# Interleaved column walks in ten of the sixteen gate projections of a hybrid encoder layer

## The chip, the cores and the metric

The kernel runs on one core of one Trainium2 chip. The metric is the device time of one execution in microseconds (us), the median over several runs. Engines are named as in the profile: PE is TensorE's matmul, PEld its weight load, DVE is VectorE, ACT is ScalarE, POOL is GpSimd, SP is SyncE.

## The reference, cut to what matters

One layer over 512 tokens of width 1024: a SwiGLU half step, a mixer with two attention branches, and a second SwiGLU half step. The change touches one part of the mixer, the gates:

```
proj = h @ w_in
pa, pq, pk, pv, pg = proj[..., :o1], proj[..., o1:o2], proj[..., o2:o3], proj[..., o3:o4], proj[..., o4:]
...
gates = jax.nn.sigmoid((pg + b_gate).reshape(B, S, N_BRANCHES, D))
merged = gates[:, :, 0] * (o_a @ w_branch_a) + gates[:, :, 1] * (o_b @ w_branch_b)
return merged @ w_out
```

`pg` has 2048 features for each of the 512 tokens. The kernel makes them as sixteen tiles of 128 features by 512 tokens.

## The kernel before, in words

**Layout.** Activations lie transposed, with features on the 128 partitions and the 512 tokens along the row. The normed input `h` stands in SBUF as eight pairs of tiles `hH[k]`, `hL[k]` (128x512 each): a value rounded to fp32r and the rest, so that a product of near fp32 accuracy is made of three fp32r matmuls. `mm3` (L248 to L252) issues these three: high weights by `hH` (L250), high weights by `hL` (L251), low weights by `hH` (L252). Weights pass through `prep`, which makes a high part `wh` on ACT (L235) and a low part `wl` on DVE (L236).

**A gate projection.** `feat` (L260 to L268) takes one PSUM bank `mm` (128x512 fp32) and one chunk of weights (128x1024, eight slices of 128 columns). For each of the eight `k` it calls `mm3`, so that 24 matmuls accumulate in the bank. In each the weights' slice is the stationary operand, `hH[k]` or `hL[k]` with its 512 columns is the moving one, and the output is the whole bank. At the end `done` (L686 to L689) multiplies the bank by the token scale `R` on DVE (L688, result `z`) and stores `z` to DRAM (`gate_d`), from where it is read back much later, after the attention (L1140). `feat` also serves the first projections of the FFNs and four query/key projections; these calls pass no walk.

**Where the gates stand.** The PE's instruction order is written out by hand (a manual schedule for PE). `self.items` lists the mixer's projections: the value projection `("v", 1)`, gates 0 to 3, the query/key block, `("v", 2)`, gates 4 and 5, two query/key pairs, gates 6 to 12, the inputs of the second attention in three groups, gates 13 to 15, and the projection of the first attention's output. The items after the query/key block are a filler stream: `weave` lets the attention issue a step and then takes a number of steps from that stream, one `mm3` each. So gates 0 to 3 stand in one piece, and gates 4 to 15 are mostly cut into pieces between attention matmuls.

**Operands that are read or written with a step.** Three places of the kernel before do not walk a row from left to right without gaps. The value projections 1 and 2 use as stationary operand every fourth column of `hH` and `hL`, `t[:, r:T:4]` (128 columns, 16 bytes from one to the next). In `values_a`, stages 2 and 3, the matmuls of L912 write every fourth column of the bank, `out[:, r0 + u // 2:T:4]`, where stages 0 and 1 write 64 or 128 columns side by side. The broadcast of one column in `stat_R` (L423) has step zero. No moving operand has a step other than one.

**Alignment.** Weight tiles are placed at a chosen offset in bytes modulo 256 (`offset`, used in `ring`). For gates the weights then start at the same place modulo 256 as `hH` and `hL` do.

Of the kernel before, what the change touches and what calls it, by code (L numbers as in the profile page):

```python
# [32 lines left out]
LAG = 1  # L33
LAST = 2
WARM = 4
T = 512
D = 1024
NK = 8
# [32 lines left out]
class Layer:  # L71
    def __init__(self, ctx, tc, a):
# [10 lines left out]
        c = self.cst  # L83
        self.x = [c.tile([128, T], F32, name=f"x{d}") for d in range(NK)]
        self.par = c.tile([128, 48], F32, name="par")
# [7 lines left out]
        self.r = c.tile([128, 8], F32, name="r")  # L93
        self.R = c.tile([128, T], F32, name="R")
        nc.gpsimd.memset(self.R, 0.0)
        self.acc = c.tile([128, T], F32, name="acc")
        self.open_h()
        self.gate_d = self.dram.tile([16, 128, T], F32, name="gate_d")
        self.qk_d = self.dram.tile([2 * NSQ, 128, T], F32, name="qk_d")
        gates = lambda lo, hi: [("g", j) for j in range(lo, hi)]  # L100
# [41 lines left out]
    def open_h(self):  # L142
        self.hctx = ExitStack()
        hp = self.hctx.enter_context(self.tc.tile_pool(name="hp", bufs=1, side="right", reuse_waits="tile"))
        self.hH = [hp.tile([128, T], F32R, name=f"hH{d}") for d in range(NK)]
        self.hL = [hp.tile([128, T], F32R, name=f"hL{d}") for d in range(NK)]
# [110 lines left out]
    def aux(self, name):  # L257
        return self.psa.tile([128, T], F32, tag="aux", name=name)

    def feat(self, name, n, done):  # L260
        ps = self.bank()
        H, L = self.weights(name, n)
        for k in range(NK):
            s = slice(128 * k, 128 * k + 128)
            self.mm3(ps, H[:, s], L[:, s], self.hH[k], self.hL[k], k == 0, k == NK - 1)
            if k == NK - 1:
                done(ps)
            yield  # L268
# [390 lines left out]
    def stream(self, items):  # L659
        nc = self.nc  # L660
        for kind, n in items:
            if kind == "v":
                toks = [(lambda t, r=r: t[:, r:T:4]) if n else (lambda t, r=r: t[:, 128 * r:128 * r + 128]) for r in range(4)]

                def done(j, b, g=n):
                    rc = self.r[:, j + (4 if g else 0):j + (5 if g else 1)]
                    if j % 2:
                        nc.vector.tensor_scalar(self.V[g][:, j, :], b, rc, None, op0=ALU.mult)
                    else:
                        nc.scalar.activation(self.V[g][:, j, :], b, AF.Copy, scale=rc)  # L670

                yield from self.token("wav", 4 * n, toks, done)
            elif kind == "qk":
                hp, g = PAIRS[n]
                for part in range(2):

                    def done(ps, hp=hp, part=part, g=g):
                        t = self.qk[hp][part, g] = self.ap.tile([128, T], F32, tag="qk", name="qk", bufs=9)
                        nc.vector.tensor_mul(t.rearrange("p (r m) -> p r m", r=4),
                                             ps.rearrange("p (m r) -> p r m", r=4),  # L680
                                             self.acc.rearrange("p (r m) -> p r m", r=4))

                    yield from self.feat("waq", 2 * n + part, done)
            elif kind == "g":

                def done(ps, j=n):  # L686
                    z = self.tmp.tile([128, T], F32, tag="t", name="z")
                    nc.vector.tensor_mul(z, ps, self.R)  # L688
                    nc.sync.dma_start(self.gate_d[j], z)  # L689

                yield from self.feat("wg", n, done)
            elif kind == "pa":
                self.ma = [self.mp.tile([128, T], F32, name=f"ma{d}") for d in range(NK)]
                for d in range(NK):
                    ps = self.bank()
                    for k in range(4):
                        self.mm3(ps, *self.block("wpa", 4 * d + k), self.oH[k], self.oL[k], k == 0, k == 3)
                        if k == 3:
                            nc.scalar.copy(self.ma[d], ps)
                        yield  # L700
            else:
                toks = [(lambda t, i=i: t[:, 128 * i:128 * i + 128]) for i in range(4)]
                yield from self.token("wb", 4 * n, toks, lambda i, b, grp=n: self.rope(grp, i, b))
                self.turn()
            self.past.add((kind, n))
# [457 lines left out]
    def layer(self, out):  # L1163
# [4 lines left out]
        warm = self.aux("warm")  # L1168
        for _ in range(WARM):
            nc.tensor.matmul(warm[:, :256], self.R[:, :128], self.R[:, :256], start=True, stop=True)  # L1170
# [125 lines left out]
```

## Time and profile before

| what | value |
|---|---|
| median of 3 runs | 1258.35 us |
| lowest and highest run | 1258.33, 1259.05 us |
| span of the profiled execution | 1257.3 us |
| its time outside the span, against the median | 1258.35 - 1257.3 = 1.05 us |
| PE matmul busy | 1244.8 us, 99% of the span, 8076 rows |
| PE weight load busy | 1112.6 us, 88% |
| DVE, ACT, POOL busy | 893.0, 595.9, 122.5 us |
| mean granted TensorE clock | 0.998 |
| HBM traffic | 170.55 MB read, 15.29 MB written |

The page gives the profiled execution its span and no other time, so the median stands in for it. The duration of a matmul row reaches from its start to its modelled end and overlaps the next row; what a matmul costs a full PE is the distance from one start to the next. An fp32 matmul that is no transpose has two rows in the trace, an fp32r matmul one.

### The profile page before, as it was taken

How to read it: one execution, taken by the hardware profiler on the slowest of the kernel's cores; microseconds unless marked ns; L12 is line 12 of the kernel's file. 1: busy time of each engine (PE TensorE's matmuls, PEld its weight loads, DVE VectorE, ACT ScalarE, POOL GpSimd, SP SyncE). 2: the span in 40 equal slices, each digit the busy share in tenths (PEclk: the TensorE clock that was granted, in tenths of full speed). 3: DMA queues.
4: the chain of work that ended last, by engine and by line, in shares of the span. 5: the costliest groups of instructions: out<-in, count | busy, mean ns of one | idle time of the engine just before them, and what ended most of it. 6: DMA issues, size and time to landing. Idle time of an engine off the chain costs nothing.

```text
span 1257.3 us, 20126 instructions
## 1 busy us (share of the span) xinstructions
PE 1244.8 (99%) x8076; PEld 1112.6 (88%) x8076; DVE 893.0 (71%) x1344; ACT 595.9 (47%) x886; POOL 122.5 (10%) x128
## 2 busy tenths in 40 slices
PE   9999999999999999999999999999999999999997
PEld 7897999899899999977788878888889989988997
DVE  7784688478784887466746798866678747874874
ACT  8551355145453444444423446654475415532553
POOL 1111101000210110200000110000301000100001
PEclk9999999999999999999999999999999999999999
DMA  9875777342385973653223220147737536743222
GB/s 296 230 192 166 193 197 192 99 103 68 135 226 180 231 222 110 218 158 101 79 97 116 85 93 17 34 150 219 225 102 187 174 100 177 193 151 102 67 84 67
DMA packets 85981, 183.49 MB, mean 146 GB/s; under 512 B 12528, under 2 KB 19072, under 8 KB 85888
## 3 DMA queue, kind: packets, MB, share of 16 engines
q1 hardware_dynamic: 68048, 141.27, 33.6%
q0 software_dynamic: 17120, 40.39, 16.1%
q8 instruction: 63, 1.03, 0.4%
q10 hardware_dynamic: 720, 0.55, 0.1%
q14 instruction: 30, 0.25, 0.1%
HBM read 170.55 MB, written 15.29 MB: 148 GB/s over the span
## 4 chain that ended last, share of the span: by engine, by line
PE 96%; DVE 1%; DMA 1%; ACT 1%; SPq 0%; issue 0%; POOL 0%; DVEq 0%
PE mm L250 25%; PE mm L252 24%; PE mm L251 24%; PE Y L251 4%; PE Y L250 4%; PE Y L252 4%; PE X L251 2%; PE X L252 2%; PE X L250 2%; PE S L861 1%; PE mm L912 1%; PE Tb L1051 1%; PE T L930 1%; PE Sb L252 1%; PE Sb L251 1%; PE Sb L250 1%
## 5 line engine op out<-in xcount | busy, mean ns | idle before, releaser
L235 ACT CAST wh<-wr 128x1024 fp32r<-128x1024 f32 x139 | 145.7, 1049 | 189.5 <-PE mm L251 125.3
L236 DVE TENSOR_TENSOR wl<-wr,wh 128x1024 fp32r<-128x1024 f32 x139 | 170.7, 1229 | 43.2 <-ACT wh L235 43.0
L250 PE MATMUL mm<-hH,wh 128*128 128x256 f32 (+1 forms) x600 | 199.6, 333 | 0.2 <-ACT hH L389 0.2
L252 PE MATMUL mm<-hH,wl 128*128 128x256 f32 (+1 forms) x600 | 195.6, 326 | 1.0 <-DVE wl L236 1.0
L251 PE MATMUL mm<-hL,wh 128*128 128x256 f32 (+1 forms) x600 | 195.5, 326 | 0.3 <-DVE hL L390 0.3
L250 PE MATMUL mm<-gg,wh 128*128 128x512 f32 (+1 forms) x376 | 141.5, 376 | 0.0
L251 PE MATMUL mm<-gg,wh 128*128 128x512 f32 (+1 forms) x376 | 141.0, 375 | 0.0
L252 PE MATMUL mm<-gg,wl 128*128 128x512 f32 (+1 forms) x376 | 141.0, 375 | 0.0
L250 PEld LDWEIGHTS mm<-hH,wh 128*128 128x128 f32 x600 | 112.8, 188 | 14.6 <-issue 3.2
L252 PEld LDWEIGHTS mm<-hH,wl 128*128 128x128 f32 x600 | 112.7, 188 | 12.0 <-DVE wl L236 1.5
L251 PEld LDWEIGHTS mm<-hL,wh 128*128 128x128 f32 x600 | 112.9, 188 | 9.8 <-DVE hL L390 0.8
L235 ACT CAST wh<-wa 128x1024 fp32r<-128x1024 f32 x50 | 52.6, 1052 | 102.8 <-PE mm L251 55.4
L235 ACT CAST wh<-wt 128x1024 fp32r<-128x1024 f32 x50 | 52.6, 1052 | 71.1 <-PE mm L251 46.4
L236 DVE TENSOR_TENSOR wl<-wt,wh 128x1024 fp32r<-128x1024 f32 x50 | 61.2, 1224 | 33.2 <-ACT wh L235 32.4
L235 ACT CAST wh<-ws 128x1024 fp32r<-128x1024 f32 x50 | 52.6, 1052 | 66.6 <-PE mm L251 47.5
L250 PE MATMUL mm<-TH,wh 128*128 128x256 f32 x304 | 83.9, 276 | 0.0
L251 PE MATMUL mm<-TL,wh 128*128 128x256 f32 x304 | 83.9, 276 | 0.0
L252 PE MATMUL mm<-TH,wl 128*128 128x256 f32 x304 | 83.9, 276 | 0.0
L250 PEld LDWEIGHTS mm<-gg,wh 128*128 128x128 f32 x376 | 70.6, 188 | 14.2 <-PE mm L252 0.9
L252 PEld LDWEIGHTS mm<-gg,wl 128*128 128x128 f32 x376 | 70.6, 188 | 12.8
L251 PEld LDWEIGHTS mm<-gg,wh 128*128 128x128 f32 x376 | 70.6, 188 | 12.5
L546 DVE TENSOR_TENSOR u<-mm,R 128x512 f32<-128x512 f32 x40 | 27.6, 691 | 75.6 <-PE mm L252 75.5
(270 smaller groups left out, 3215.7 us busy)
## 6 DMA issues: line engine op xcount, KB each, us to landing
wr<-in_w2a SPq DMA_DIRECT2D x22, 512.0 KB, 3.4
wr<-in_w2b SPq DMA_DIRECT2D x22, 512.0 KB, 3.4
wt<-in_w13b SPq DMA_DIRECT2D x20, 512.0 KB, 3.4
wa<-in_w13b SPq DMA_DIRECT2D x20, 512.0 KB, 3.3
wt<-in_w13b POOLq DMA_DIRECT2D x20, 512.0 KB, 5.8
wt<-in_w13a SPq DMA_DIRECT2D x18, 512.0 KB, 3.5
wt<-in_w13a POOLq DMA_DIRECT2D x18, 512.0 KB, 6.1
wa<-in_w13a SPq DMA_DIRECT2D x18, 512.0 KB, 3.3
```

What stands on the lines that cost most here:

```text
L235: self.nc.scalar.copy(H, raw)
L236: self.nc.vector.tensor_sub(L, raw, f32(H))
L250: mm(out, lH, rH, start=start, stop=False, skip_group_check=more)
L251: mm(out, lH, rL, start=False, stop=False, skip_group_check=more)
L252: mm(out, lL, rH, start=False, stop=stop, skip_group_check=more)
L546: nc.vector.tensor_mul(u, ps, R)
L861: nc.tensor.matmul(*args, start=True, stop=True)
L912: nc.tensor.matmul(oc, v, p, start=st, stop=sp)
L930: nc.tensor.transpose(ps[:, 128 * b:128 * b + 128], P[h][:, c0 + 128 * b:c0 + 128 * b + 128], self.ident)
L1051: nc.tensor.transpose(pt[:, 128 * j:128 * j + 128], P[h, j][:, 128 * k:128 * k + 128], self.ident)
```

## The change

A table gives ten of the gates a pair (parts, run); gates 0, 5, 10, 11, 12 and 15 have none. (The title that came with the change speaks of eleven gates; the table holds ten.) For a gate with a pair, moving operand and output are handed to the matmul as the same 512 columns in another order: the row is cut into `parts` equal parts, and the walk takes `run` neighbouring columns from the first part, `run` from the second, and so on, and then the next runs. With (2, 2) the columns come in the order 0, 1, 256, 257, 2, 3, 258, 259 and so on. Both sides use one order, so that each column of the output still gets its own sum. Number and order of the instructions, weights, tiles and waits stay as they were.

```
WALK = {1: (2, 2), 2: (2, 4), 3: (2, 8), 4: (2, 16), 6: (2, 32), 7: (2, 64), 8: (4, 16), 9: (4, 4), 13: (8, 8), 14: (2, 128)}
...
+    @staticmethod
+    def walk(t, how):
+        if how is None:
+            return t
+        parts, run = how
+        return t.rearrange("p (a m c) -> p m a c", a=parts, c=run)
+
-    def feat(self, name, n, done):
+    def feat(self, name, n, done, how=None):
...
-            self.mm3(ps, H[:, s], L[:, s], self.hH[k], self.hL[k], k == 0, k == NK - 1)
+            self.mm3(self.walk(ps, how), H[:, s], L[:, s], self.walk(self.hH[k], how), self.walk(self.hL[k], how), k == 0, k == NK - 1)
...
-                yield from self.feat("wg", n, done)
+                yield from self.feat("wg", n, done, WALK.get(n))
```

On PE, at the seam between gate 1 and gate 2 (both in the first piece, before the query/key block), there stands before, output on the left of the arrow, then moving and stationary operand, then the moving operand's shape:

```order
L250 MATMUL mm<-hH_104,wh 128x512
L251 MATMUL mm<-hL_112,wh 128x512
L252 MATMUL mm<-hH_104,wl 128x512
L250 MATMUL mm<-hH_97,wh 128x512
L251 MATMUL mm<-hL_105,wh 128x512
```

and now:

```order
L251 MATMUL mm<-hH_104,wh 128x128x2x2
L252 MATMUL mm<-hL_112,wh 128x128x2x2
L253 MATMUL mm<-hH_104,wl 128x128x2x2
L251 MATMUL mm<-hH_97,wh 128x64x2x4
L252 MATMUL mm<-hL_105,wh 128x64x2x4
```

No row has moved; the 512 columns are now read as 128 times 2 parts times runs of 2 in gate 1, and as 64 times 2 times 4 in gate 2. (The line numbers inside `mm3` are one higher because the table stands above it.)

Further on, on PE in the woven part, where gate 8 ends and gate 9 begins between two steps of the first attention (L912 before, L920 now, are the products of probabilities and values), there stands before:

```order
L912 MATMUL mm<-PT,V_3443 64x128 x8
L250 MATMUL mm<-hH_104,wh 128x512
L251 MATMUL mm<-hL_112,wh 128x512
L252 MATMUL mm<-hH_104,wl 128x512
L250 MATMUL mm<-hH_97,wh 128x512
```

and now:

```order
L920 MATMUL mm<-PT,V_3443 64x128 x8
L251 MATMUL mm<-hH_104,wh 128x8x4x16
L252 MATMUL mm<-hL_112,wh 128x8x4x16
L253 MATMUL mm<-hH_104,wl 128x8x4x16
L251 MATMUL mm<-hH_97,wh 128x32x4x4
```

Here too the neighbours are the same, and only the shapes of the gate's matmuls differ. On PE 240 rows differ in this way, 24 for each of ten gates; on DVE, ACT, POOL and SP none differs.

More of the change, by code (lines that the diff above doesn't have):

```diff
@@ L35 @@
 WARM = 4
+WALK = {1: (2, 2), 2: (2, 4), 3: (2, 8), 4: (2, 16), 6: (2, 32), 7: (2, 64), 8: (4, 16), 9: (4, 4), 13: (8, 8), 14: (2, 128)}
 T = 512
```

## The prediction

> **What bounds the kernel now.** I read the page first, then PE's waits, then the places at which gates stand, and last the rows that show a step in an operand. The page says that PE is the bound:
>
> ```profile
> span 1257.3 us, 20126 instructions
> PE 1244.8 (99%) x8076; PEld 1112.6 (88%) x8076; DVE 893.0 (71%) x1344; ACT 595.9 (47%) x886; POOL 122.5 (10%) x128
> PE 96%; DVE 1%; DMA 1%; ACT 1%; SPq 0%; issue 0%; POOL 0%; DVEq 0%
> ```
>
> PE is busy for 99% of the span, and 96% of the chain that ended last is PE. PE's waits leave nothing to be won or to hide in:
>
> ```profile
> PE mm L912 <- DVE PT L932: 1.5, 1, 1.5
> PE warm L1170 <- POOL R L95: 1.3, 1, 1.3
> PE mm L252 <- DVE wl L236: 1.0, 1, 1.0
> PE rb L423 <- POOL r L407: 1.0, 1, 1.0
> PE stat L414 <- ACT sqh L624: 0.5, 1, 0.5
> PE mm L251 <- DVE PTL L158: 0.4, 1, 0.4
> PE mm L251 <- DVE hL L390: 0.3, 1, 0.3
> PE mm L250 <- ACT hH L389: 0.2, 1, 0.2
> PE Tb L1051 <- DVE Pb L1045: 0.2, 1, 0.2
> ```
>
> Together they are 6.4 us, nine waits in the whole span. So what a gate's matmul costs PE is added to the end in full, and what it saves is taken off in full.
>
> What a gate costs is read where gates 0 to 3 stand in one piece. These are DVE's rows there; each `z` starts when its gate's last matmul is done:
>
> ```profile
> 377.53 0.69 DVE L688 TENSOR_TENSOR z<-mm,R 128x512 f32<-128x512 f32 x1 [2.77 <-PE mm L252]
> 382.97 0.69 DVE L688 TENSOR_TENSOR z<-mm,R 128x512 f32<-128x512 f32 x1 [3.31 <-PE mm L252]
> 388.41 0.69 DVE L688 TENSOR_TENSOR z<-mm,R 128x512 f32<-128x512 f32 x1 [3.36 <-PE mm L252]
> 393.85 0.69 DVE L688 TENSOR_TENSOR z<-mm,R 128x512 f32<-128x512 f32 x1 [3.36 <-PE mm L252]
> ```
>
> A gate takes 5.44 us from `z` to `z`, and has 24 matmuls, so a matmul costs 5440/24 = 226.7 ns, whatever its row's duration is. That is 0.443 ns for one column of 4 bytes, and 226.7/128 = 1.77 ns for four neighbouring columns, 16 bytes of a partition. DVE waits about 3.3 us in front of each `z`, so it is no bound there.
>
> **The change part by part.** Nothing is removed or added; 240 matmuls (ten gates by 24) read and write the same columns in another order. DMAs, weights, DVE and ACT work and all waits are the same. So the sum has one price in it, the distance between such matmuls, times 240, and nothing hides it. It has three parts: the moving operand's reads, the output's writes, and how the reads stand against the next weights' load.
>
> *The reads.* The trace before has no moving operand with a step, so I take the nearest row, a stationary operand with one. In this window the weight loads of the value projection take one column out of four (16 bytes from one to the next), and beside them are weight loads without a step:
>
> ```profile
> L251 PEld LDWEIGHTS mm<-wl,hH 128*128 128x128 f32 x13 | 4.0, 311 | 0.0
> L250 PEld LDWEIGHTS mm<-wh,hH 128*128 128x128 f32 x13 | 4.0, 310 | 0.0
> L252 PEld LDWEIGHTS mm<-wh,hL 128*128 128x128 f32 x13 | 4.0, 309 | 0.0
> L251 PEld LDWEIGHTS mm<-gg,wh 128*128 128x128 f32 x10 | 1.9, 188 | 0.4
> ```
>
> The step costs 310 - 188 = 122 ns for 128 columns, 0.95 ns a column. What a column costs without a step comes from loads of fewer columns, here 8 columns and 64:
>
> ```profile
> L650 PEld LDWEIGHTS bps<-bias,rel_bias x6: 80/82/84, 101.0 to 109.5; 32*8 32x8 f32 x6
> ```
>
> ```profile
> L912 PEld LDWEIGHTS mm<-PT,V x256: 132/137/138, 558.2 to 655.9; 128*64 128x64 f32 x128
> ```
>
> From 64 to 128 columns it is (188 - 137)/64 = 0.80 ns a column, from 8 to 128 (188 - 82)/120 = 0.88 ns. With the step a column costs 0.80 + 0.95 = 1.75 to 0.88 + 0.95 = 1.83 ns. So one column out of 16 bytes takes as long as the moving operand needs for 16 whole bytes, 1.77 ns. I read this as a port that takes 16 bytes at a time, about 1.77 ns each, and a plain moving operand that is already at that limit.
>
> By this a walk pays for each visit to a new group of 16 bytes. Runs of 4 and more start at multiples of 16 bytes (`hH` and `hL` start at a multiple of 32 bytes, and the parts are 256, 512 or 1024 bytes long): such a walk visits 128 groups a matmul, as the plain one does, and costs nothing. Gate 1 alone, with runs of 2, uses half of each group and comes back later for the rest: 512/2 = 256 visits by 1.77 ns = 453 ns in place of 226.7. For its 24 matmuls that is 24 x 226.7 ns = **5.44 us** more; with 1.75 to 1.83 ns a visit, 5.3 to 5.8 us. The lower bound for gate 1 is zero, if two columns are enough to hide the next visit; a gain I exclude, since the plain order already has the fewest visits. For the other nine gates the lower bound is zero too. Their upper bound is one lost visit at every jump: their runs are 128 + 128 + 64 + 64 + 32 + 32 + 16 + 8 + 4 = 476 a matmul, times 24 times 1.77 ns = 20.2 us. I take zero, by the loads with the step, which jump at every column and still pay no more than a visit.
>
> [...]
>
> *The writes.* The nearest rows are the products of L912 in `values_a`. The first of these two is stage 0, with columns side by side, the second stage 2, with every fourth column of the bank, both accumulating:
>
> ```profile
> 558.19 1.09 PE L912 MATMUL mm<-PT,V 128*64 128x128 f32 x16
> ```
>
> ```profile
> 569.26 1.09 PE L912 MATMUL mm<-PT,V 128*64 128x128 f32 x16 [1.51 <-DVE PT L932]
> ```
>
> The same 16 rows take 1.09 us either way, so a step of 16 bytes in the output costs nothing here. These are fp32 matmuls of 128 columns, slower for each column than a gate's, so it is no proof for 0.443 ns a column. I take zero; the upper bound is a matmul of double length, as a rival below.
>
> [...]
>
> *Against the weights' load.* In the value projection the weights are read with a step while the moving operand runs plainly, and the matmuls stand a little wider:
>
> ```profile
> 354.19 0.40 PE L252 MATMUL mm<-wh,hL 128*128 128x512 f32 x1
> ...
> 357.01 0.40 PE L252 MATMUL mm<-wh,hL 128*128 128x512 f32 x1
> ```
>
> There are twelve steps between the two (the rows run L250, L251, L252 four times): 2.82/12 = 235 ns, 8 ns over a gate's 226.7. A walk changes how the moving reads stand against the next weights' reads, so it can lose as much: 0 to 240 x 8 ns = 1.9 us. I take the 72 matmuls of gates 1 to 3, which are at 226.7 ns now: 72 x 8 ns = **0.6 us**. The other seven stand among attention steps, where the distance varies already.
>
> The sum against the profiled execution is 1257.3 + 5.44 + 0.6 = 1263.3 us of span; with the 1.05 us that lie outside it, 1258.35 + 6.0 = **1264.4 us**. The later parts have no cover to lose: gate 1's DVE row and its store come 5 us later, and the next items have their weights ready, as PE's waits show none there.
>
> **The rivals.** *Two columns are enough.* Not slower than before: the port fetches the next 16 bytes while two columns are used, so that 1.77 ns a visit is a latency and not a rate. It decides in gate 1, and wins if a matmul there stays under 240 ns. For it: the stepped loads show one column a visit only, never two. Against it: plain moving columns already go at 1.77 ns for four. Time: 1258.35 + 0 to 1.9, say 1258.9 us. Chance 0.30.
>
> *Every jump costs.* The port takes more than 16 bytes ahead when a row is read in order, and a jump throws that away. Half a visit a jump, 0.89 ns x 476 x 24 = 10.1 us, beside gate 1's 5.44: 1273.9 us. For it: moving reads run in order everywhere before, so no row excludes it. Against it: the stepped loads, whose columns are at least in ascending order, show no more than a visit. Chance 0.16.
>
> *The output pays.* All ten gates write jumping at full rate, and their matmuls double: 240 x 226.7 ns = 54.4 us, 1312.8 us. For it: L912 writes fewer columns in a given time. Against it: its equal 1.09 us. Gate 14, with only four runs a matmul, would show it by itself. Chance 0.08.
>
> *The walks part the two reads better.* If the walks took away the 8 ns in the seven woven gates and cost nothing else, 168 x 8 ns = 1.3 us would go: 1257.0 us. Chance 0.04. That the walk is lost on its way to the engine can be left out, since the shapes of 240 PE rows carry it.
>
> **How the numbers follow.** My forecast has 0.42, with a range of its own from 1261 us (half of gate 1's price) to 1266.2 (5.8 and 1.9 us more). The range for 8 in 10 goes from the last rival's 1257.0 to the 1273.9 of the jumps: it holds the forecast, the first rival, the last one, and half of the jumps, 0.42 + 0.30 + 0.04 + 0.08 = 0.84, less a little at the edges. A measurement of this kernel can tell about 0.2%, 2.5 us, from no change. Faster than that would take twice the last rival's price; I give it half of that rival's chance, 0.02. Within it lie the first rival and the other half, 0.32; slower are 0.42 + 0.16 + 0.08 = 0.66.
>
> **What would show it.** Right: gate 1 takes about 10.9 us from the `z` of gate 0 to its own, gates 2 and 3 about 5.4 to 5.6 us each, and gates 4 to 15 as long as before. Wrong: gate 1 at 5.4 us means the first rival; gates 2 and 3 at rising prices for shorter runs (gate 2 at twice gate 3's surplus) mean the jumps; gate 14 longer by over 1 us means the output. PE's waits should stay where they are.

## The result, and the profile after

| | before | after |
|---|---|---|
| median of 3 runs | 1258.35 us | 1263.79 us |
| lowest and highest run | 1258.33, 1259.05 | 1263.76, 1264.39 |
| ratio, 95% interval | | 1.0042, 1.0027 to 1.0057 |
| span of the profiled execution | 1257.3 us | 1262.0 us |

The kernel is 5.44 us slower, where 6.0 was forecast. That is more than 0.2%, and the forecast lies inside the interval. The total hides two errors, though: gate 1 costs 2.7 us where 5.44 were forecast, and the other nine gates cost 2.8 us where almost nothing was. These are the lines of the page after that answer to those of before:

```profile
span 1262.0 us, 20126 instructions
PE 1249.9 (99%) x8076; PEld 1112.5 (88%) x8076; DVE 893.0 (71%) x1344; ACT 596.5 (47%) x886; POOL 122.7 (10%) x128
PE 96%; DMA 1%; ACT 1%; DVE 1%; SPq 0%; issue 0%; POOL 0%; POOLq 0%; DVEq 0%
```

The span grew by 4.7 us and PE's busy time by 5.1; the other engines' busy times moved by 0.6 us at most, and the mean granted clock is 0.998 in both. The spans differ by less than the medians do. In the profiled execution after, 1263.79 - 1262.0 = 1.8 us lie outside the span, and in the runs below it is about as much; so the 1.05 us that the median gave for before set its span against the wrong time, and the profiled execution of before was probably the 1259.05 us one. PE's longest waits after, with total, count and longest in us:

```profile
PE warm L1178 <- POOL R L96: 1.3, 1, 1.3
PE mm L920 <- DVE PT L940: 1.1, 1, 1.1
PE rb L431 <- POOL r L415: 1.0, 1, 1.0
PE mm L253 <- DVE wl L237: 1.0, 1, 1.0
```

They are the first four of nine. All nine are the same as before, 6.0 us together in place of 6.4. So no new wait came in, and the loss is in the distance between matmuls. DVE's rows for gates 0 to 3, each `z` after its gate's last matmul:

```profile
377.35 0.69 DVE L696 TENSOR_TENSOR z<-mm,R 128x512 f32<-128x512 f32 x1 [2.77 <-PE mm L253]
385.50 0.69 DVE L696 TENSOR_TENSOR z<-mm,R 128x512 f32<-128x512 f32 x1 [6.02 <-PE mm L253]
391.51 0.69 DVE L696 TENSOR_TENSOR z<-mm,R 128x512 f32<-128x512 f32 x1 [4.00 <-PE mm L253]
397.34 0.69 DVE L696 TENSOR_TENSOR z<-mm,R 128x512 f32<-128x512 f32 x1 [3.77 <-PE mm L253]
```

From `z` to `z` gate 1 takes 8.15 us, gate 2 6.01, gate 3 5.83. By 24 matmuls that is 340, 250 and 243 ns each, all from 226.7. The woven gates are read between two rows with nothing but matmuls of one gate between them. PE's rows in gate 9, walk (4, 4), before:

```profile
626.47 0.40 PE L250 MATMUL mm<-hH,wh 128*128 128x512 f32 x1
...
627.84 0.39 PE L250 MATMUL mm<-hH,wh 128*128 128x512 f32 x1
```

and after:

```profile
630.17 0.43 PE L251 MATMUL mm<-hH,wh 128*128 128x512 f32 x1
...
630.98 0.44 PE L251 MATMUL mm<-hH,wh 128*128 128x512 f32 x1
```

Before, six steps take 1.37 us, 228 ns each; after, three take 0.81 us, 270 ns each. The table gives the mean over all rows of a gate that are followed by another fp32r matmul; the last column is 24 times the difference.

| gate | walk (parts, run) | ns before | ns after | us in all |
|---|---|---|---|---|
| 1 | (2, 2) | 226.7 | 339.2 | 2.70 |
| 2 | (2, 4) | 226.7 | 250.5 | 0.57 |
| 3 | (2, 8) | 226.7 | 243.3 | 0.40 |
| 4 | (2, 16) | 252.8 | 260.5 | 0.18 |
| 6 | (2, 32) | 238.8 | 246.4 | 0.18 |
| 7 | (2, 64) | 246.5 | 246.2 | -0.01 |
| 8 | (4, 16) | 243.8 | 245.5 | 0.04 |
| 9 | (4, 4) | 238.5 | 275.6 | 0.89 |
| 13 | (8, 8) | 231.2 | 253.1 | 0.53 |
| 14 | (2, 128) | 239.0 | 238.5 | -0.01 |

The sum is 5.47 us, and gate 1 has half of it. That the medians differ by nearly the same 5.44 us is in part luck: the two executions from which the rows come differ by 4.7 us. Of the 0.8 us between, the waits explain 0.4 and the time ahead of gate 0's `z` 0.2.

### The profile page after: what moved, and what is told of

Its sections match the earlier page's. It is cut to its first block, busy times and chain, and to the rows that moved or that the text cites. A ratio compares the mean times of both kernels' runs of the same rounds, so it can differ in the third digit from the quotient of the medians.

```text
span 1262.0 us, 20126 instructions
## 1 busy us (share of the span) xinstructions
PE 1249.9 (99%) x8076; PEld 1112.5 (88%) x8076; DVE 893.0 (71%) x1344; ACT 596.5 (47%) x886; POOL 122.7 (10%) x128
## 4 chain that ended last, share of the span: by engine, by line
PE 96%; DMA 1%; ACT 1%; DVE 1%; SPq 0%; issue 0%; POOL 0%; POOLq 0%; DVEq 0%
PE mm L251 25%; PE mm L253 24%; PE mm L252 24%; PE Y L251 4%; PE Y L252 4%; PE Y L253 4%; PE X L251 2%; PE X L252 2%; PE X L253 2%; PE S L869 1%; PE mm L920 1%; PE Tb L1059 1%; PE T L938 1%; PE Sb L253 1%; PE Sb L252 1%; PE Sb L251 1%
## 5 line engine op out<-in xcount | busy, mean ns | idle before, releaser
L253 PEld LDWEIGHTS mm<-gg,wl 128*128 128x128 f32 x376 | 70.6, 188 | 12.8
```

Source lines behind the costliest of these rows:

```text
L253: mm(out, lL, rH, start=False, stop=stop, skip_group_check=more)
```

## The experiments

**Which operand, and which gate.** Three kernels on one chip; the kernel before had a median of 1259.15 us there. The first walks the moving operand alone, the second the output alone (the columns of ten gates come out in another order in both), and the third does the whole change without gate 1.

reads_only:

```
-            self.mm3(self.walk(ps, how), H[:, s], L[:, s], self.walk(self.hH[k], how), ...
+            self.mm3(ps, H[:, s], L[:, s], self.walk(self.hH[k], how), ...
```

> The ten walked gates read their moving operand in walked order and write the bank in plain order, so their columns come out permuted. If the moving reads carry the price: gate 1 stays at about 340 ns a matmul, gate 2 at 250, gate 3 at 243, gate 9 near 275, and the time is 5.4 us over the kernel before, as with the change (1263.8 us). If the output's writes carry it: all ten gates are back at 227 to 247 ns and the time is that of before within 1 us. If both carry a part, gate 1 lies between.

Measured: 1263.99 us, ratio 1.0038 (1.0025 to 1.0052). DVE's rows:

```profile
377.42 0.69 DVE L696 TENSOR_TENSOR z<-mm,R 128x512 f32<-128x512 f32 x1 [2.77 <-PE mm L253]
385.58 0.69 DVE L696 TENSOR_TENSOR z<-mm,R 128x512 f32<-128x512 f32 x1 [6.02 <-PE mm L253]
391.58 0.69 DVE L696 TENSOR_TENSOR z<-mm,R 128x512 f32<-128x512 f32 x1 [4.00 <-PE mm L253]
```

Gates 1 and 2 take 8.16 and 6.00 us, as with the whole change: the reads carry the loss. (On this chip it is 4.84 us, which the interval of the change, 3.4 to 7.2 us, holds.)

writes_only:

```
-            self.mm3(self.walk(ps, how), H[:, s], L[:, s], self.walk(self.hH[k], how), self.walk(self.hL[k], how), ...
+            self.mm3(self.walk(ps, how), H[:, s], L[:, s], self.hH[k], self.hL[k], ...
```

> The ten walked gates read plainly and write the bank in walked order, so their columns come out permuted. If the moving reads carry the price: no gate differs from before (gate 1 at 227 ns) and the time is that of before within 1 us. If the writes carry it: gate 1 at 340 ns, +5.4 us.

Measured: 1259.10 us, ratio 1.0000 (0.9991 to 1.0009). DVE's rows:

```profile
377.38 0.69 DVE L696 TENSOR_TENSOR z<-mm,R 128x512 f32<-128x512 f32 x1 [2.77 <-PE mm L253]
382.82 0.69 DVE L696 TENSOR_TENSOR z<-mm,R 128x512 f32<-128x512 f32 x1 [3.31 <-PE mm L253]
388.26 0.69 DVE L696 TENSOR_TENSOR z<-mm,R 128x512 f32<-128x512 f32 x1 [3.36 <-PE mm L253]
```

Gate 1, which writes runs of 2 from two halves of the bank, takes 5.44 us from `z` to `z`, as before. Writing in these orders cost nothing at full rate: 1259.10 us beside 1259.15. Single columns are not tested by this kernel, since no run is shorter than 2.

no_gate1:

```
-WALK = {1: (2, 2), 2: (2, 4), 3: (2, 8), ...
+WALK = {2: (2, 4), 3: (2, 8), ...
```

> The change without gate 1's walk (runs of 2); nine gates walk. By the prediction gate 1 carries nearly all: the time would be 1258.4 to 1259.0 us. By the matmul distances of the changed kernel's trace gate 1 carries 24 x (339 - 227) ns = 2.7 us and the other nine 2.8 us: about 2.8 us over before, some 1261.1 us.

Measured: 1261.55 us, ratio 1.0018 (1.0010 to 1.0027), 2.4 us over the kernel before. DVE's rows:

```profile
376.98 0.69 DVE L696 TENSOR_TENSOR z<-mm,R 128x512 f32<-128x512 f32 x1 [2.77 <-PE mm L253]
382.42 0.69 DVE L696 TENSOR_TENSOR z<-mm,R 128x512 f32<-128x512 f32 x1 [3.31 <-PE mm L253]
388.43 0.69 DVE L696 TENSOR_TENSOR z<-mm,R 128x512 f32<-128x512 f32 x1 [3.90 <-PE mm L253]
```

Gate 1 is back at 5.44 us, and gate 2 keeps its 6.01. So the nine gates cost 2.4 us by themselves, near the 2.8 of their rows, and the prediction's claim that gate 1 carries nearly all of it fell.

**One price a jump, or not.** To see each walk without attention between its matmuls, thirteen projections that stand in one piece got a walk each, in both operands (four first projections of the first FFN, gates 0 to 3 and 5, four first projections of the second FFN).

sweep_both:

```
+WALK = {('w13a', 4): (8, 2), ('w13a', 5): (2, 2), ('w13a', 6): (2, 4), ...
...
+    def feat(self, name, n, done):
+        how = WALK.get((name, n))
```

> Both operands walk, in thirteen projections that stand in one piece, so that each distance is read undisturbed; plain is 226.7 ns. Parts x run: 8x2, 2x2, 2x4, 2x8 in the last four plain projections of the first FFN, 2x16, 2x32, 2x64, 2x128 in gates 0 to 3, 4x2 in gate 5, 4x4, 4x8, 8x4, 8x8 in the plain projections of the second FFN. If a walk pays for each visit of 16 bytes and nothing else: 340 ns for all three with runs of 2, 227 for all others. If each jump pays: the distance falls with the run alone, the same for 2, 4 and 8 parts (4x4 and 8x4 like 2x4 at 250, 4x8 and 8x8 like 2x8 at 243). If the moving reads and the next weights' load collide: runs of 4 and more depend on the number of parts as well (4x4 near 265, 2x4 at 250), and on nothing beyond a run of 64.

The distances are read from one execution. PE's rows of the second to the eighth `k` in the projections with (8, 2) and then (2, 2):

```profile
32.48 0.67 PE L251 MATMUL mm<-hH,wh 128*128 128x512 f32 x1
...
41.24 0.67 PE L251 MATMUL mm<-hH,wh 128*128 128x512 f32 x1
...
43.70 0.50 PE L251 MATMUL mm<-hH,wh 128*128 128x512 f32 x1
...
49.60 0.50 PE L251 MATMUL mm<-hH,wh 128*128 128x512 f32 x1
```

There are 18 steps in each pair of rows: 8.76/18 = 487 ns for (8, 2) and 5.90/18 = 328 ns for (2, 2). All walks, as the mean of the sixteen distances in the middle of a projection (the same in the other tables below):

| run | 2 parts | 4 parts | 8 parts |
|---|---|---|---|
| 2 | 328.0 | 443.3 | 486.7 |
| 4 | 250.0 | 268.3 | 277.8 |
| 8 | 243.3 | 231.1 | 250.1 |
| 16 | 240.0 | | |
| 32 | 236.7 | | |
| 64 | 228.1 | | |
| 128 | 226.7 | | |

Over 226.7, and divided by the runs of a matmul, the surplus is 0.18 ns a run at (2, 4), 0.33 at (4, 4), 0.07 at (4, 8), 0.63 at (2, 32). So there is no one price for a jump; run and number of parts (the distance that a jump goes) both count. At (2, 64) only the first distances are longer, and the later ones are 226.7 ns. Neither visits alone nor jumps alone gave this table beforehand; the sign named for a collision of reads and loads, (4, 4) near 265 beside (2, 4) at 250, did come, and it is put to the test next.

**Does the weights' load collide with the walk?** Two kernels. In the first the middle six of eight `k` load 8 weight columns, or 64, in place of 128 (the rest of those sums is left out); in the second the weights start 64, 128 or 192 bytes (modulo 256) behind the moving tile.

narrow_weights:

```
+            c = how[2] if how and 0 < k < NK - 1 else 128
+            w = slice(128 * k, 128 * k + c)
+            self.mm3(self.walk(ps, how)[:c], H[:, w], L[:, w], ...
```

> Thirteen undisturbed projections as in the sweep, but the six middle steps k = 1 to 6 load 8 weight columns in place of 128 (64 in the last two), so that sums are left out for the other output rows; the weights' reads are all but gone there. Plain control 1x512; then 2x2, 2x4, 2x8, 4x2, 8x2, 4x4, 8x8, 2x16, 8x4, 2x32, and 2x2, 2x4 with 64 weight columns. If the walk pays by itself (visits or jumps): the same distances as with 128 columns, 2x2 at 328 to 340, 2x4 at 250, 2x8 at 243, 4x2 at 445, 8x2 at 487, 4x4 at 268, 8x4 at 279, 8x8 at 250 ns. If the surplus of runs of 4 and more is a collision of the two reads: 2x4, 2x8, 2x16, 4x4, 8x4, 8x8 fall to the control's 227 ns within 2, and with 64 columns 2x4 lies about half way; runs of 2 keep what is the visits' own.

PE's rows with 8 weight columns in the projection with (2, 2):

```profile
38.35 0.50 PE L251 MATMUL mm<-hH,wh 128*8 128x512 f32 x1
...
42.27 0.50 PE L251 MATMUL mm<-hH,wh 128*8 128x512 f32 x1
```

3.92 us for 12 steps, 326.7 ns, beside 328.0 with all the weights. The other walks: (4, 2) 443.4, (8, 2) 486.6, (2, 4) 246.2, (4, 4) 265.9, (8, 4) 277.7, (2, 8) 242.2, (8, 8) 244.1, (2, 16) 240.0, (2, 32) 236.6; no walk 226.7. With 64 columns, in two projections of the second FFN, (2, 4) has 246.7, but (2, 2) 346.7, more than with 8 or 128. With 8 weight columns in place of 128, 0 to 6 ns of a walk's surplus go, and no more.

weights_moved:

```
     def offset(self, n):
         name, key = self.order[n][:2]
+        if (name, key) in WALK:
+            return (224 + WALK[name, key][2]) % 256
```

> Both operands walk, but the weights start 64, 128 or 192 bytes (modulo 256) behind the moving tile in place of 0. 2x4 at 64, 128, 192; 4x4 at 64, 128, 192; 2x2 at 64, 128; 2x16 at 128; plain at 128; 2x16 at 64; 2x8 at 128 and 64. If the surplus is a collision of the two reads: distances change with the offset by several ns, 2x4 to between 227 and 250 at some offset, plain at 128 up to 231 or 236. If it is a price of jumps or visits: 250, 268, 328 to 340, 240, 243 ns as at offset 0.

DVE's rows for gates 0 to 2; gate 1 walks (4, 4) with the weights at 192, gate 2 walks (2, 2) with the weights at 64:

```profile
381.28 0.69 DVE L699 TENSOR_TENSOR z<-mm,R 128x512 f32<-128x512 f32 x1 [3.75 <-PE mm L255]
387.73 0.69 DVE L699 TENSOR_TENSOR z<-mm,R 128x512 f32<-128x512 f32 x1 [4.33 <-PE mm L255]
395.58 0.69 DVE L699 TENSOR_TENSOR z<-mm,R 128x512 f32<-128x512 f32 x1 [5.79 <-PE mm L255]
```

6.45 and 7.85 us, 269 and 327 ns a matmul, as in the sweep. (2, 4) has 251.6, 250.0 and 248.4 at 64, 128 and 192; (4, 4) 268.8 to 269.1 at all three. The plain order reacts too: 232.0 at 128, in a projection where the same sixteen distances average 228.1 in the kernel before. So most of a walk's surplus lies in the moving reads themselves. Not all of it is settled, for (2, 2) is not one number: it has 340.0 ns in gate 1 of the changed kernel and 328.0 in the sweep's FFN projection, both with the kernel's usual offset, and 326.6 and 326.7 in gates 2 and 3 with the weights moved. Up to 13 ns of gate 1's surplus of 113 may thus hang on how the weights stand; no run moves gate 1's weights with this walk.

**Runs in ascending order.** If a visit to 16 bytes has one price, a walk that takes the first 2 columns of each 4 from left to right, and then the other 2, must cost what I predicted for gate 1. The next kernel does this with several steps and runs, in the reads alone (columns come out in another order); its companion also has 8 weight columns in the middle six `k`.

steps_read:

```
-        return t.rearrange("p (a m c) -> p m a c", a=parts, c=run)
+        return t.rearrange("p (m h c) -> p h m c", h=parts, c=run)
```

> The same thirteen projections with another order of the reads alone (output plain, its columns permuted): the row is gone through in order, taking runs of c columns at a step of h x c, then again for the next runs. No group of 16 bytes is visited twice soon after. Step x run in columns: 4x2, 8x2, 16x2, 32x2; 8x4, 16x4, 32x4, 64x4; 4x1, 2x1; 16x8, 64x8, 32x8. If each visit of 16 bytes costs about 1.77 ns: all four with runs of 2 at 453 ns, 4x1 (512 visits) at 907, 2x1 (two columns of a group in a row) at 453, all with runs of 4 and 8 at 227. If two columns of a group are enough and the price lay in going back and forth between parts: the ascending runs of 2 at 227. If the place within 256 bytes counts: a step of 64 columns (64x4) is the dearest of the runs of 4, near 280, and 8x4 the cheapest.

PE's rows: first, pairs out of every 4 columns; then single columns out of every 4:

```profile
32.18 0.63 PE L251 MATMUL mm<-hH,wh 128*128 128x512 f32 x1
...
40.34 0.63 PE L251 MATMUL mm<-hH,wh 128*128 128x512 f32 x1
```

```profile
571.71 0.64 PE L251 MATMUL mm<-hH,wh 128*128 128x512 f32 x1
...
580.02 0.64 PE L251 MATMUL mm<-hH,wh 128*128 128x512 f32 x1
```

18 steps each: 453.3 and 461.7 ns. The first is the predicted price to the nanosecond. The second refutes the reason that I gave for it: single columns make 512 visits, which by 1.77 ns would be 907 ns. All of them in one table, ns a matmul; rows are the columns taken together, columns the distance from one run's start to the next:

| run | 8 B | 16 B | 32 B | 64 B | 128 B | 256 B |
|---|---|---|---|---|---|---|
| 1 | 451.1 | 461.3 | | | | |
| 2 | | 453.3 | 461.4 | 431.1 | 462.9 | |
| 4 | | (plain: 226.7) | 233.3 | 225.2 | 247.2 | 279.2 |
| 8 | | | (plain: 226.7) | 232.4 | 231.1 | 250.1 |

A group of 16 bytes read whole costs 0.44 to 0.55 ns a column; read in pieces, in ascending order, every column costs 0.84 to 0.90 ns, whether pieces of one or two. Among whole groups the distance to the next one counts: for runs of 4, 64 bytes are the best (225.2 ns) and 256 the worst (279.2) of those tried. Every run of 4 or more here starts at a multiple of 16 bytes; a run of 4 that starts in the middle of a group was not tried, so whether the group or the length of the run sets the price is not shown. Runs of 1 at 8 B and runs of 2 at 16 B read two columns of a group in a row and pay double (451.1 and 453.3 ns), so two are not enough for this operand; four are, where the distance suits (225.2 ns at 64 B).

steps_narrow:

```
+            c = 8 if how and 0 < k < NK - 1 else 128
```

> As the run with steps, with 8 weight columns in steps k = 1 to 6 (sums left out there). If the surplus of runs of 4 and 8 is a collision with the weights' reads: they go to 227 ns whatever the step, and runs of 2 show the bare price of a visit, 453 ns, or less if a visit is cheaper than 1.77 ns. If it is a price of jumps: no change against the run with 128 weight columns.

Measured: runs of 1 451.1 (8 B) and 460.0 (16 B); runs of 2 451.1, 460.7, 430.0, 433.3; runs of 4 230.8, 221.4, 245.1, 278.3; runs of 8 229.9 (64 B), 231.3 (128 B), 225.1 (256 B). Two of them fell by more than 5 ns: runs of 2 at 128 B, from 462.9, and runs of 8 at 256 B, from 250.1. There the load does seem to take part; in the others 3.8 ns go at most, so the price is that of the reads.

**Gate 1 in ascending order.** The same in the changed kernel itself, both operands, against the kernel before (1259.19 us on this chip).

gate1_ascending:

```
         parts, run = how
+        if run == 2:
+            return t.rearrange("p (m a c) -> p a m c", a=parts, c=run)
```

> The changed kernel, but gate 1 takes its runs of 2 in ascending order (columns 0, 1, 4, 5, 8, 9 and so on, then 2, 3, 6, 7), in both operands, so that a group of 16 bytes is not met again soon. If each visit costs 1.77 ns and going back and forth between two parts is what made gate 1 cheaper: 453 ns a matmul there, 24 x (453 - 339) = 2.7 us over the changed kernel, about 1266.5 us against 1258.4 to 1259.2 of before, the loss that the prediction gave gate 1. If runs of 2 cost the same in any order: 340 ns and 1263.8 us.

Measured: 1267.35 us, ratio 1.0063 (1.0049 to 1.0076). DVE's rows:

```profile
377.70 0.69 DVE L698 TENSOR_TENSOR z<-mm,R 128x512 f32<-128x512 f32 x1 [2.77 <-PE mm L253]
388.58 0.69 DVE L698 TENSOR_TENSOR z<-mm,R 128x512 f32<-128x512 f32 x1 [8.75 <-PE mm L253]
394.60 0.69 DVE L698 TENSOR_TENSOR z<-mm,R 128x512 f32<-128x512 f32 x1 [4.12 <-PE mm L253]
```

Gate 1 takes 10.88 us, where 10.9 was predicted for the change. The kernel is 8.16 us slower than the kernel before, where the change was 5.44 slower: 2.7 us more, as 24 x (453 - 340) ns gives. The number of visits is the same 256 in both. They differ in when the second half of a group is asked for: after one other group with (2, 2), after all 128 here. With 4 and 8 parts three and seven other groups lie between, and 443 and 487 ns are about as dear as the ascending order. But the length of the jumps changes with it: 1024 bytes to and fro with (2, 2), 512 and 256 with 4 and 8 parts, 16 here. Which of the two makes (2, 2) cheaper was not tested apart.

**The order that is faster than the plain one.** Runs of 4 at 64 bytes came out at 225.2 ns, under the plain 226.7. The next kernel tries them with the weights at several offsets, and longer runs, with both operands walked; two more use them for every fp32r matmul of 512 columns (2904 of them).

more_walks:

```
+WALK = {('w13a', 4): (4, 4, 0), ('w13a', 5): (4, 4, 64), ('w13a', 6): (4, 4, 128), ('w13a', 7): (4, 4, 192), ...
...
+        return t.rearrange("p (m h c) -> p h m c", h=parts, c=run)
```

> Both operands walk in ascending order with a step. Step x run in columns: 16x4 with the weights at offset 0, 64, 128, 192; 32x16, 64x16, 64x32, 128x64, 128x32, 128x8; 16x4 with offset 32; 128x16; 16x4 with offset 96. If the distance to the next group of 16 bytes sets the price and 64 bytes is the best distance: 16x4 between 220 and 227 ns at every offset, below plain's 226.7; runs of 16 and more within 10 ns of plain. If the 225 ns of the run before were chance: 226 to 236.

Measured for runs of 4 at 64 bytes, by the weights' offset: 0 223.3, 32 227.1, 64 226.6, 96 226.8, 128 225.3, 192 220.0 ns. Here offset and walk do act together. Runs of 16 have 240.0 at 128 and 256 B and 231.1 at 512; runs of 32 have 236.6 at 256 B and 233.4 at 512; runs of 64 228.2 at 512; runs of 8 at 512 231.2. None of these longer runs is under the plain order. The 240.0 lies further from it than the 10 ns that were expected.

all_walk:

```
+        if rH.shape[-1] == 512 and len(rH.shape) == 2:
+            out, rH, rL = (self.walk(t, (4, 4)) for t in (out, rH, rL))
         mm(out, lH, rH, start=start, stop=False, skip_group_check=more)
```

> Every fp32r matmul with 512 moving columns (2904 of them) walks in steps of 16 columns with runs of 4, in both operands. If such a walk is 1.5 ns shorter than the plain one wherever it stands: 2904 x 1.5 ns = 4.4 us less than before, about 1254.5 us. If it only moved collisions with the weights' reads: within 2 us of before; if other moving tiles lie worse: some us slower.

Measured: 1252.12 us, ratio 0.9945 (0.9932 to 0.9957): 7.07 us less, 2.4 ns a matmul, and more than the 4.4 us expected. The gain does not come from the gates that stand in one piece, which take 5.45 and 5.42 us, beside 5.44 before:

```profile
375.89 0.69 DVE L699 TENSOR_TENSOR z<-mm,R 128x512 f32<-128x512 f32 x1 [2.76 <-PE mm L255]
...
381.34 0.69 DVE L699 TENSOR_TENSOR z<-mm,R 128x512 f32<-128x512 f32 x1 [3.33 <-PE mm L255]
...
386.76 0.69 DVE L699 TENSOR_TENSOR z<-mm,R 128x512 f32<-128x512 f32 x1 [3.35 <-PE mm L255]
```

In the second FFN the matmuls with moving operand `gg` went from 226.8 to 223.6 ns on average.

all_walk_moved (the same, with the weights 192 bytes behind the moving tile, modulo 256):

```
-            return 96
-        return 160 if name in ("w2a", "w2b", "wpa", "wpb", "wo") else 224
+            return 32
+        if name in ("wav", "wb"):
+            return 224 if name == "wav" else 32
+        return 96 if name in ("w2a", "w2b", "wpa", "wpb", "wo") else 160
```

> As the run in which every 512-column fp32r matmul walks in steps of 16 columns with runs of 4, and the weights that such matmuls load start 192 bytes (modulo 256) behind the moving tile in place of 0, where they can (not for the value projection's stepped loads, nor the scores). If the offset of 192 gives a steady 220 ns wherever it stands, as in the one projection that showed it, in place of the 224 to 227 of the run before: some 2500 matmuls by 4 to 6 ns, 10 to 15 us less than that run, 1237 to 1242 us against 1259 of before. If that projection owed its 220 ns to its place: 1250 to 1254 us as in the run before.

Measured: 1246.36 us beside 1259.12, ratio 0.9904 (0.9887 to 0.9920), between the two outcomes that were expected. The page's first lines, and DVE's rows for three gates:

```profile
span 1243.4 us, 20140 instructions
...
PE 1230.2 (99%) x8076; PEld 1112.8 (89%) x8076; DVE 893.5 (72%) x1344; ACT 594.7 (48%) x886; POOL 122.0 (10%) x128
```

```profile
373.57 0.69 DVE L701 TENSOR_TENSOR z<-mm,R 128x512 f32<-128x512 f32 x1 [2.63 <-PE mm L257]
378.85 0.69 DVE L701 TENSOR_TENSOR z<-mm,R 128x512 f32<-128x512 f32 x1 [3.15 <-PE mm L257]
384.13 0.69 DVE L701 TENSOR_TENSOR z<-mm,R 128x512 f32<-128x512 f32 x1 [3.20 <-PE mm L257]
```

A gate takes 5.28 us, 24 times 220.0 ns. The gain of 12.8 us by 2904 matmuls is 4.4 ns each, less than 6.7: the last four first projections of the first FFN, for example, have 223.3 with the same walk and offset. One of them had 220.0 in more_walks, and why it differs here is not known. PE is still the bound. This version beats both kernels.

## Why the prediction was right, and where it was not

**Direction and total: right.** PE has no slack (99% of the span before and after), so what a matmul costs more is added to the end. The span grew by 4.7 us and PE's waits stayed. That the total came within 0.6 us is luck: gate 1's term was too large by 2.7 us, and the nine gates' and alignment terms together too small by 2.2.

**"512/2 = 256 visits by 1.77 ns = 453 ns in place of 226.7": the step that failed.** Gate 1 measured 339 ns, so the term of 5.44 us was 2.70. The 453 ns are the price of pairs in ascending order (453.3 in the step study, 10.88 us for gate 1). The alternating order, with the same 256 visits, pays about half of that surplus. And the unit was wrong: singles in ascending order cost 461 ns and not 907. In ascending order it is a column of a group read in pieces that costs about 0.89 ns, not a visit that costs 1.77; for pairs the two readings give the same number, so that the 453 ns of pairs are no proof of the visit. The stepped weight loads could not give the price either. They read single columns at 16 bytes, for which the moving operand pays 461/512 = 0.90 ns a column, half of the 1.75 to 1.83 read from the loads; and the 310 ns were the length of rows that overlap, as PEld's rows before show:

```profile
353.96 0.31 PEld L252 LDWEIGHTS mm<-wh,hL 128*128 128x128 f32 x1
354.20 0.31 PEld L250 LDWEIGHTS mm<-wh,hH 128*128 128x128 f32 x1
```

They start 0.24 us apart and last 0.31, so their length is not a rate. What agrees between the operands, by these lengths, is rather the factor, about two over the plain column of each (0.80 to 0.88 ns there, 0.443 here).

**"I take zero, by the loads with the step, which jump at every column": failed.** The nine gates cost 2.8 us by their rows, 2.4 by the run without gate 1. Those loads jump 16 bytes ahead each time; the walks jump 256, 512 and 1024 bytes back and forth, and whole groups of 4 columns cost more there (277.8, 268.3 and 250.0 ns in the sweep, and 279.2 at 256 bytes in ascending order, beside 233.3 at 32). So "gates 4 to 15 as long as before" failed as well, by 0.89 us in gate 9 and 0.53 in gate 13. The bounds, zero to 20.2 us, held it. "A gain I exclude, since the plain order already has the fewest visits" did not hold for walks in general: the 64-byte order has the same 128 visits and takes 220.0 ns at best.

**The term of 0.6 us for how reads and the next weights' load stand: failed as it was reasoned.** No run shows 8 ns in each of gates 1 to 3. With 8 weight columns (2, 4) and (2, 8) lose 3.8 and 1.1 ns of surpluses of 23 and 17, and up to 13 ns of (2, 2) may hang on the weights' place. By these numbers the load's part is at most 24 x (13 + 3.8 + 1.1) ns = 0.4 us, an estimate. Gates 2 and 3, named at 5.4 to 5.6 us, took 6.01 and 5.83, mostly for the order of their reads.

**The writes at zero: right,** now shown at full rate for these ten walks, ratio 1.0000.

**The rivals.** "Two columns are enough" asked for gate 1 under 240 ns; it has 339. "Every jump costs" is right that most jumps cost, but not in its price: it gave gate 2 128 x 0.89 = 114 ns more, and 24 were measured, and its sign, gate 2 at twice gate 3's surplus, did not come (24 and 17 ns). The port of 16 bytes, in the forecast and in these two, is the author's reading of the loads; no run shows it. "The output pays" is out: gate 14 did not move (239.0 and 238.5 ns), and the output's walk alone cost nothing (1259.10 us beside 1259.15); no run shows the matmuls of double length behind its 54.4 us, which were the author's assumption. "The walks part the two reads better" did not happen in this change, but something like it exists: the 64-byte order with moved weights gains 6.7 ns a matmul.

**Open.** Why runs of 2 are cheaper to and fro over 1024 bytes (339 ns in gate 1) than in ascending order (453): the runs show that they are, not whether it is the early return to a group or the length of the jump. Why (2, 2) has 340 ns in gate 1 and 327 or 328 elsewhere. Why 64 bytes are the best distance tried (225.2 ns in the step study), what the plain order loses between 220.0 and 226.7 ns, and why 64 weight columns made (2, 2) dearer (346.7 ns).

## What to carry to other kernels

Here, with PE busy for 99% of the span, the order in which a matmul walked its moving columns was a cost of its own, from 220.0 to 487 ns for the same 512 columns. Where PE is the bound of another kernel, try runs of 4 columns or more from a multiple of 16 bytes first (220.0 to 279 ns here; runs of 1 and 2 took 327 to 487), and mind the distance to the next run (225.2 ns at 64 bytes and 279.2 at 256, for runs of 4). The order in which the output is written was free in the ten walks tried by themselves here (1259.10 us beside 1259.15). A price taken from another operand (a stepped weight load) should be split into what it was measured on, column, visit and distance, before it is carried over. And a total that comes out right is no proof of its terms: the rows gate by gate, then gate 1 left out and gate 1 in another order, showed that two of them were wrong.

## What was not expected of the hardware

The plain order is not the fastest. With runs of 4 columns at 64 bytes from one to the next and the weights 192 bytes (modulo 256) behind the moving tile, an fp32r matmul of 512 columns takes 220.0 ns in place of 226.7 in gates 0 to 3 (223.3 in four first projections of the first FFN), and the whole kernel 0.9904 of its time. The plain order itself changed with where the weights start: in one projection 228.1 ns at the same place modulo 256, 232.0 at 128 bytes behind it. Eight parts by runs of 2 cost 487 ns, more than any ascending order tried.
